# Reordering the side work of a delta-rule recurrence across the three phases of each step

## The chip, the cores and the metric

The kernel runs on one core of a Trainium2 chip. The metric is the device time of one execution in microseconds; where several runs are given, their median counts. A profiled execution also has a span, from the first to the last instruction in its trace, which is a little shorter than the time of the execution.

## The reference, cut to what matters

The reference is one post-norm encoder layer over 2048 tokens of 1024 channels. A single input projection feeds a gated long convolution (FFT) and an RWKV-7 mixer; the two are gated, projected and normed, and a SwiGLU network follows. The change lies in the RWKV-7 part, a recurrence over tokens that is run once in each direction:

```
def rwkv_step(S, inp):
    r, w, k, v, kk, a = inp
    sa = einsum('dbhvk,dbhk->dbhv', S, -kk)
    S = S * w[..., None, :] + sa[..., :, None] * (kk * a)[..., None, :] + v[..., :, None] * k[..., None, :]
    y = einsum('dbhvk,dbhk->dbhv', S, r)
    return S, y
...
_, ys = lax.scan(rwkv_step, S0, xs)
```

There are 8 heads with a 64 x 64 state each. The two directions are summed, normed per head, given a bonus term and a gate.

## The kernel before, in words

The kernel's stages follow one another on the core: projection of most columns with the preparation of the recurrence's operands beside it, then the recurrence (`chain`), the long convolution (`hyena`), the merge, and the feed-forward network. The projection's last 88 column blocks are kept back and computed inside the recurrence, as filler for TensorE; they are called the dense work here (tile `acc`, lines 202 to 204). One dense unit is three matmuls of 512 columns, and eight units make a block.

The recurrence works on chunks of 64 tokens: 32 chunks in each direction, N = 64 steps, in 8 groups of 8 steps (`g`, `st = divmod(n, 8)`). A step has three dependent products on TensorE, each followed by a copy on another engine:

- R: `pR` (line 803), the chunk's inputs against the state; ScalarE copies it to `R` (line 806). The step before then has its output product `pY` issued (`output`, lines 841 and 843).
- S: `pS` (line 816), the inverse `X` of the chunk's triangular matrix times `R`; ScalarE copies it to `SV` (line 819).
- D: `pD` (line 825), the state's change; VectorE adds and decays it into the next state (lines 831 and 832), which the next step's R needs.

`step` is a generator that yields after the R, the S and the D product. After each yield, `runs` issues some dense units (a share of the step's dense time: 0, a half, a half) and some of the step's side work, the parts that `beside` lists:

- `token_major(n + 1)`: four transposes for the next step's D (`pT`, line 786).
- `gram(g + 1, k)`: for each of the next group's eight chunks, 16 matmuls into two PSUM tiles of the tag `pg` (`pG`, line 677), then four masked copies on VectorE (line 656). Its input `ABp` is a DMA into one of three buffers, asked for when the third gram before it has been issued (line 667). Four grams stand in step 0 of a group and four in step 1 (`GRAMS`).
- `finish(g, hb)`: the correction that completes half of a group's inverses. A first product `pW1` (line 726) reads `XT` and the Gram tile `G`, two copies take it to `w1` (lines 733 and 734), and a second product `pW2` (line 739) reads `w1` and `X`. Half 0 (chunks 0 to 3) of the next group is finished in step 7, half 1 (chunks 4 to 7) in step 0 of the group itself. Half 0 also issues `states` for the next group's first chunk after `pW1`: two DMAs on SyncE's queue into `G` (line 781) that the first R of that group reads.
- `gated` (`pgg`, line 910) and `channel_major` (`pgt`, line 878): the output path, in the second direction alone.

All PSUM tiles of the side work share the tag `pg`, which has three buffers. The side work's parts are one list, and each phase runs down the list by cost: 0.34, 0.33 and 0.33 of the step's estimated cost, and what is left after the third. A step's dense time is a level minus the estimated cost of its side work (`share`), so that all steps come out about equally long.

After step 0 `gather(g + 1, 0)` and after step 1 `gather(g + 1, 1)` send the two halves of the Gram tiles through DRAM (GpSimd's queue, line 691). After step 1 `invert(g + 1)` follows: it loads `N` (line 701), runs a chain of 31 pairs of VectorE operations (lines 706 and 708), transposes the result into `XT` (line 713) and sends it through DRAM into `X` (lines 714 and 717). `XT` and `N` share one buffer.

The order of TensorE's instructions is the order in which the program issues them. The other engines' and the queues' order is planned when the program is built, by program order and the priorities given (`high_priority`).

The last three steps (n = 61 to 63; LAST is 61) have no dense work. At n = 61 `open` issues the loads for the convolution stage, and `step(61)` then issues `fetch(63)`, the last chunk's operands (`BK`, line 754); in steps 62 and 63 the side list ends with a part of the convolution's filters (`taps`, tiles `pg` and `pf`).

Of the kernel before, what the change touches and what calls it, by code (L numbers as in the profile page):

```python
# [25 lines left out]
NCH = L // CH  # L26
# [6 lines left out]
AHEAD = 1500  # L33
FIRST = 500
RUSH = 400
GRAMS = ((0, 1, 2, 3), (4, 5, 6, 7))
FX = 2
TB = 256

# [150 lines left out]
class Layer:  # L190
# [431 lines left out]
    def chain(self):  # L622
        tc, nc, i = self.tc, self.nc, self.i
        mm, tt, ts = nc.tensor.matmul, nc.vector.tensor_tensor, nc.vector.tensor_scalar
        NG, N = 8, 2 * NCH
        with tc.tile_pool(name="ch", bufs=1, reuse_waits="tile") as s, tc.tile_pool(name="chp", bufs=1, space=PSUM, reuse_waits="tile") as ps:
# [18 lines left out]
            def place(n):  # L645
                d, m = divmod(n, NCH)
                return d, (m if d == 0 else NCH - 1 - m)
# [72 lines left out]
            def finish(g, hb):  # L720
                G, XT, X = grp[g]["G"], grp[g]["XT"], Xs[g % 2]
                sl = slice(16 * hb, 16 * hb + 16)
                p1 = pg("pW1", (P, 16, 32))
                for n in range(16):
                    for j in range(2):
                        mm(p1[dn[j], n], G[up[j], j, 16 * hb + n, 32:64], XT[up[j], 16 * hb + n], start=True, stop=True)
                yield 0.55
                if g and hb == 0:
                    for j in range(2):
                        states(g * NG, j)  # L730
                w1 = s.tile([P, 16, 32], F32, name="w1", tag="w1", bufs=1)
                with tc.high_priority(offset=AHEAD):
                    nc.scalar.copy(w1[dn[0]], p1[dn[0]])
                    nc.vector.tensor_copy(w1[dn[1]], p1[dn[1]])
                yield 1.0
                p2 = pg("pW2", (P, 16, 32))
                for n in range(16):
                    for j in range(2):
                        mm(p2[up[j], n], w1[dn[j], n], X[dn[j], 16 * hb + n, 32:64], start=True, stop=True)
                yield 0.55  # L740
                with tc.high_priority(offset=AHEAD):
                    nc.scalar.copy(X[up[0], sl, 32:64], p2[up[0]])
                    nc.vector.tensor_copy(X[up[1], sl, 32:64], p2[up[1]])

            ins, VSs, T2s = {}, {}, {}
# [37 lines left out]
            def token_major(n):  # L783
                p = pg("pT", (P, HP, P))
                for hp in range(HP):
                    nc.tensor.transpose(p[:, hp], ins[n][0][:, hp], self.ident)
                    yield 0.11
                T2s[n] = s.tile([P, HP, P], F32, name="T2", tag="T2", bufs=2)
                with tc.high_priority(offset=AHEAD):
                    nc.scalar.copy(T2s[n], p)  # L790


            def step(n):
                d, c = place(n)
                g, st = divmod(n, NG)
                G, Gr, X = grp[g]["G"], grp[g]["Gr"][st], Xs[g % 2]
                BK, SV = ins.pop(n)
                VS = VSs.pop(n)
                T2 = T2s.pop(n)
                p = ps.tile([P, HP, 64], F32, name="pR", tag="pc", bufs=1)  # L800
                for hp in range(HP):
                    for j in range(2):
                        mm(p[opp[j], hp], G[:, j, HP * st + hp], VS[:, j, hp], start=True, stop=True)
                R = s.tile([P, HP, 64], F32, name="R", tag="R", bufs=1)
                with tc.high_priority(offset=AHEAD):
                    nc.scalar.copy(R, p)

                if late:
                    output(*late.pop())
                if n + 2 < N:  # L810
                    fetch(n + 2)
                yield 0.0, 0.34
                p = ps.tile([P, HP, 64], F32, name="pS", tag="pc", bufs=1)
                for hp in range(HP):
                    for j in range(2):
                        mm(p[opp[j], hp], X[opp[j], HP * st + hp], R[opp[j], hp], start=True, stop=True)
                with tc.high_priority(offset=AHEAD):
                    for j in range(2):
                        nc.scalar.copy(SV[opp[j], j], p[opp[j]])
                late.append((n, VS, SV, Gr))  # L820
                yield 0.5, 0.33
                pd = ps.tile([P, HP, 64], F32, name="pD", tag="pD", bufs=1)
                for hp in range(HP):
                    for j in range(2):
                        mm(pd[opp[j], hp], T2[:, hp, row[j]], SV[:, j, hp], start=True, stop=True)
                for j in range(2):
                    if (n + 1) % NCH == 0:
                        break
                    S1, q = VSs[n + 1][opp[j], j], opp[j]
                    with tc.high_priority(offset=AHEAD):  # L830
                        tt(out=S1, in0=pd[q], in1=VS[q, j], op=ALU.add)
                        tt(out=S1, in0=S1, in1=Dks[q, d, :, c:c + 1].broadcast_to([64, HP, 64]), op=ALU.mult)
                yield 0.5, 0.33

            def output(n, VS, SV, Gr):
                d, c = place(n)
# [111 lines left out]
            def beside(n, make=True):  # L948
                g, st = divmod(n, NG)
                parts = []  # L950
                if n + 1 < N:
                    parts.append((0.44, lambda: token_major(n + 1)))
                if n > NCH + 3 and n % 2 == 0:
                    parts.append((0.87, lambda: gated(place(n - 3)[1])))
                if g + 1 < N // NG:
                    for k in GRAMS[st] if st < len(GRAMS) else ():
                        parts.append((0.92, lambda k=k: gram(g + 1, k)))
                for hb, at in enumerate((NG - 1, 0)):
                    h = g + (at >= 4)
                    if st == at and 0 < h < N // NG:  # L960
                        parts.append((2.1, lambda h=h, hb=hb: finish(h, hb)))
                if n > NCH + 1:
                    parts.append((0.22, lambda: channel_major(place(n - 2)[1])))
                return sum(t for t, _ in parts), [f() for _, f in parts] if make else None

            costs = [beside(n, False)[0] for n in range(N)]

# [40 lines left out]

            owed = [0.0]

            def runs(need, aux, cost):
                owed[0] += need
                while need and owed[0] > 0.3:
                    t = next(more, None)
                    if t is None:
                        owed[0] = 0.0
                        break
                    left[0] -= t
                    owed[0] -= t
                while aux and cost > 0:  # L1020
                    t = next(aux[0], None)
                    if t is None:
                        aux.pop(0)
                    else:
                        cost -= t

            with tc.manual_schedule(engines={mybir.EngineType.PE}):
                begin(0)
# [18 lines left out]
                for n in range(N):  # L1047
                    g, st = divmod(n, NG)
                    if st == 0 and g + 1 < N // NG:
                        begin(g + 1)  # L1050
                    cost, aux = beside(n)
                    sh = share(n)
                    if n == LAST + 1:
                        taps = self.filt(0, 0)
                    if n >= LAST + 1:
                        aux.append(self.part(taps, 4.0))
                        cost += 4.0
                    outward(n)
                    if n > NCH + 2 and n % 2 == 1:
                        given(place(n - 2)[1])  # L1060
                    for k in range(n + 1, N if n >= LAST else min(n + 2, N)):
                        if k not in VSs:
                            near(k)
                    if n == LAST:
                        self.open()
                    for dense, other in step(n):
                        runs(sh * dense, aux, cost * other)
                    runs(0.0, aux, 1e9)
                    if n == LAST - 1:
                        for _ in more:  # L1070
                            pass
                    if n >= LAST and pieces:
                        self.taken(pieces.pop(0))
                    if st < len(GRAMS) and g + 1 < N // NG:
                        gather(g + 1, st)
                        if st:
                            invert(g + 1)
                output(*late.pop())
                for part in (gated(2), channel_major(1), channel_major(0), gated(0)):
# [50 lines left out]
    def next(self, name):  # L1130
        first, n = dict(w=(8, 2), g=(10, 2), A=(12, 2), B=(0, 2), H=(2, 3), Hs=(5, 3))[name]
        k = self.turns[name]
        self.turns[name] = k + 1
        return self.ring(first + k % n).rearrange("p (a b) -> p a b", b=P)
# [580 lines left out]
```

## Time and profile before

| what | us |
|---|---|
| median of 3 runs (lowest, highest) | 4027.47 (4022.36, 4030.42) |
| profiled execution, its time | 4030.92 |
| its span | 4029.1 |
| TensorE busy in the span | 3839.9 |
| recurrence's steps 0 to 60 in the trace, from and to | 746.5 to 1570.8 |

All times in the rows are counted from the start of the span. A busy TensorE is not TensorE at its peak: matmuls are pipelined, and their ends are modelled. The granted clock of TensorE stands as a share of full speed; 1.00 is 2.4 GHz and 0.50 is 1.2 GHz.

### The profile page before, as it was taken

The page shows a single profiled execution, that of the slowest core. Times are in us where ns is not written, and L with a number is a line of the kernel's source. Part 1 is how long each engine was busy: PE and PEld are TensorE (multiplying, and loading weights), DVE is VectorE, ACT ScalarE, POOL GpSimd, SP SyncE. Part 2 cuts the span into 40 slices and gives each one's busy share as a digit, 9 for nine tenths or more (in the row PEclk, how much of TensorE's full clock was granted, in tenths as well). Part 3 has the DMA queues.
Part 4 walks back from the last instruction along what each step waited for, and adds up shares of the span by engine and source line. Part 5 has one row for each costly group of instructions (what it writes and reads, how often), then busy time and mean ns, then how long its engine had stood idle before and what let it go on. Part 6 is the DMA issues. An engine that isn't in the chain of part 4 may idle for free. (4 is left out here: it accounts for less than half of the span.)

```text
span 4029.1 us, 64417 instructions
## 1 busy us (share of the span) xinstructions
PE 3839.9 (95%) x25872; PEld 3128.8 (78%) x25872; DVE 2422.1 (60%) x3823; ACT 1486.7 (37%) x2912; POOL 93.1 (2%) x139
## 2 busy tenths in 40 slices
PE   8999999899999998898888999999999999999998
PEld 6766557777777777788887899788888877888887
DVE  4456884666667774777876665544444464444444
ACT  3345662333335566665654333211111151111113
POOL 0000001111100000000000000000000000000000
PEclk9999999999999999899999999999999999999999
DMA  4556878676767766221225333411111132111111
GB/s 138 171 166 177 218 201 241 198 214 206 213 202 217 219 195 197 62 72 49 73 71 173 127 123 121 162 48 47 48 47 48 47 130 80 47 48 47 48 47 42
DMA packets 389698, 501.84 MB, mean 125 GB/s; under 512 B 135364, under 2 KB 271053, under 8 KB 388693
## 3 DMA queue, kind: packets, MB, share of 16 engines
q1 hardware_dynamic: 362775, 443.13, 36.7%
q10 hardware_dynamic: 20736, 37.80, 3.1%
q0 software_dynamic: 5888, 16.78, 1.4%
q8 instruction: 204, 3.34, 0.3%
q14 instruction: 95, 0.78, 0.1%
HBM read 352.74 MB, written 127.93 MB: 119 GB/s over the span
## 5 line engine op out<-in xcount | busy, mean ns | idle before, releaser
L202 PE MATMUL acc<-xh,wh 128*128 128x512 f32 x1376 | 580.1, 422 | 10.8 <-ACT xh L197 10.8
L203 PE MATMUL acc<-xl,wh 128*128 128x512 f32 x1376 | 550.1, 400 | 9.8 <-DVE xl L198 9.7
L204 PE MATMUL acc<-xh,wl 128*128 128x512 f32 x1376 | 549.5, 399 | 0.4 <-DVE wl L198 0.4
L1652 DVE TENSOR_TENSOR acc<-pd,acc 128x1024 f32<-128x1024 f32 x320 | 387.7, 1221 | 70.4 <-PE pd L204 64.5
L197 ACT CAST fwh<-raw 128x1024 fp32r<-128x1024 f32 x132 | 138.6, 1050 | 705.6 <-PE pg L203 488.9
L202 PEld LDWEIGHTS acc<-xh,wh 128*128 128x128 f32 x1376 | 261.2, 190 | 125.5 <-issue 48.6
L1680 DVE TENSOR_TENSOR h<-pu,sg 128x512 f32<-128x512 f32 x88 | 60.9, 692 | 492.0 <-PE pu L204 486.0
L203 PEld LDWEIGHTS acc<-xl,wh 128*128 128x128 f32 x1376 | 262.4, 191 | 73.0 <-DVE xl L198 13.6
L204 PEld LDWEIGHTS acc<-xh,wl 128*128 128x128 f32 x1376 | 262.0, 190 | 64.2 <-DVE wl L198 0.8
L202 PE MATMUL pd<-fwh,hh 128*128 128x512 f32 x704 | 276.3, 392 | 2.6 <-DVE acc L1650 2.2
L204 PE MATMUL pu<-fxh,fwl 128*128 128x512 f32 x704 | 277.5, 394 | 0.0
L204 PE MATMUL pg<-fxh,fwl 128*128 128x512 f32 x704 | 277.3, 394 | 0.0
L203 PE MATMUL pg<-fxl,fwh 128*128 128x512 f32 x704 | 276.2, 392 | 0.0
L202 PE MATMUL pg<-fxh,fwh 128*128 128x512 f32 x704 | 276.0, 392 | 0.2 <-DVE fxl L1567 0.2
L202 PE MATMUL pu<-fxh,fwh 128*128 128x512 f32 x704 | 275.3, 391 | 0.4 <-ACT fxh L1566 0.4
L203 PE MATMUL pu<-fxl,fwh 128*128 128x512 f32 x704 | 275.8, 392 | 0.0
L203 PE MATMUL pd<-fwl,hh 128*128 128x512 f32 x704 | 275.5, 391 | 0.0
L204 PE MATMUL pd<-fwh,hl 128*128 128x512 f32 x704 | 274.8, 390 | 0.0
L198 DVE TENSOR_TENSOR fwl<-raw,fwh 128x1024 fp32r<-128x1024 f32 x132 | 161.2, 1221 | 166.4 <-ACT fwh L197 162.5
L198 DVE TENSOR_TENSOR wl<-wraw,wh 128x512 fp32r<-128x512 f32 (+1 forms) x217 | 169.8, 791 | 136.1 <-ACT wh L197 125.0
L197 ACT CAST wh<-wraw 128x512 fp32r<-128x512 f32 (+1 forms) x217 | 150.7, 705 | 235.7 <-PE acc L203 202.3
L1221 DVE STREAM_TRANSPOSE V<-U 128x1024 f32<-128x1024 f32 x96 | 181.0, 1953 | 32.9 <-ACT U L1299 12.5
(299 smaller groups left out, 7583.0 us busy)
## 6 DMA issues: line engine op xcount, KB each, us to landing
wraw<-in_w_in SPq DMA_DIRECT2D x130, 512.0 KB, 5.0
ABp<-ABd SPq DMA_DIRECT2D x64, 512.0 KB, 5.8
raw<-in_fg SPq DMA_DIRECT2D x44, 512.0 KB, 3.4
raw<-in_fu SPq DMA_DIRECT2D x44, 512.0 KB, 3.5
raw<-in_fd SPq DMA_DIRECT2D x44, 512.0 KB, 3.5
ud<-ev ACTq DMA_DIRECT2D x84, 256.0 KB, 3.0
ABd<-AB SPq DMA_DIRECT2D x32, 512.0 KB, 5.0
gated<-ev SPq DMA_DIRECT2D x64, 256.0 KB, 2.8
```

The source lines that it names most:

```text
L197: nc.scalar.copy(hi, src)
L198: nc.vector.tensor_tensor(out=lo, in0=src, in1=hi.bitcast(F32), op=ALU.subtract)
L202: mm(ps, ah, bh, start=start, stop=False)
L203: mm(ps, ah, bl, start=False, stop=False)
L204: mm(ps, al, bh, start=False, stop=stop)
L1221: self.nc.vector.transpose(V[:, :, sl].rearrange("p j c -> p c j"), U[:, :, sl].rearrange("p n c -> p c n"))
L1652: tt(out=acc[t], in0=pf, in1=acc[t], op=ALU.add)
L1680: tt(out=h, in0=put, in1=sg, op=ALU.mult)
```

## The change

Each part of the side work is given a phase of its step. `beside` returns three lists, one for each phase, and `runs` issues the phase's dense units and then the whole of the phase's list. The estimated costs still set the dense time of a step, with 1.1 for a `finish` where 2.1 stood.

- The grams are spread as 3, 3 and 2 over steps 0, 1 and 2; steps 0 and 1 have one in each phase, step 2 one in phases 0 and 2.
- `finish` loses its first yield; its first product and the copies are in phase 1, its second product in phase 2. Half 1 moves from step 0 to step 2 of its group; half 0 stays in step 7.
- `token_major` is in phase 1, `channel_major` in phase 2, `gated` in phase 1 of steps with grams and in phase 0 of the others.
- The first gather stands after step 1, the second gather and `invert` after step 2.
- At n = 61 `fetch(63)` is issued ahead of `open`.
- In steps 62 and 63 the filters' part is split over the phases (0.8, 1.7, 1.7 where 4.0 stood at the list's end).

```diff
-GRAMS = ((0, 1, 2, 3), (4, 5, 6, 7))
+GRAMS = ((0, 1, 2), (3, 4, 5), (6, 7))
...
                         mm(p1[dn[j], n], G[up[j], j, 16 * hb + n, 32:64], XT[up[j], 16 * hb + n], start=True, stop=True)
-                yield 0.55
                 if g and hb == 0:
                     for j in range(2):
                         states(g * NG, j)
...
                     nc.vector.tensor_copy(w1[dn[1]], p1[dn[1]])
-                yield 1.0
+                yield 0.55
...
-                if n + 2 < N:
+                if n + 2 < N and n + 2 not in ins:
                     fetch(n + 2)
-                yield 0.0, 0.34
+                yield 0.0
...
+                put = lambda k, t, f: parts.append((k, t, f))
+                ks = GRAMS[st] if st < len(GRAMS) and g + 1 < N // NG else ()
+                for p, k in zip((0, 2) if len(ks) == 2 else (0, 1, 2), ks):
+                    put(p, 0.92, lambda k=k: gram(g + 1, k))
+
+                for hb, at in enumerate((NG - 1, 2)):
+                    h = g + (hb == 0)
+                    if st == at and 0 < h < N // NG:
+                        f = []
+                        put(1, 0.55, lambda h=h, hb=hb: f.append(finish(h, hb)) or until(f[0], 1))
+                        put(2, 0.55, lambda: f[0])
                 if n + 1 < N:
-                    parts.append((0.44, lambda: token_major(n + 1)))
+                    put(1, 0.44, lambda: token_major(n + 1))
+                if n > NCH + 1:
+                    put(2, 0.22, lambda: channel_major(place(n - 2)[1]))
                 if n > NCH + 3 and n % 2 == 0:
-                    parts.append((0.87, lambda: gated(place(n - 3)[1])))
...
-                return sum(t for t, _ in parts), [f() for _, f in parts] if make else None
+                    put(1 if ks else 0, 0.87, lambda: gated(place(n - 3)[1]))
+                total = sum(t for _, t, _ in parts)
+                return total, [[f() for k, _, f in parts if k == p] for p in range(3)] if make else None
+
+            def until(gen, n):
+                for _ in range(n):
+                    yield next(gen)
...
-                while aux and cost > 0:
-                    t = next(aux[0], None)
-                    if t is None:
-                        aux.pop(0)
-                    else:
-                        cost -= t
+                for gen in aux:
+                    for _ in gen:
+                        pass
...
-                        aux.append(self.part(taps, 4.0))
-                        cost += 4.0
+                        for p in range(3):
+                            aux[p].append(self.part(taps, 1.7 if p else 0.8))
...
                     if n == LAST:
+                        fetch(n + 2)
                         self.open()
-                    for dense, other in step(n):
-                        runs(sh * dense, aux, cost * other)
-                    runs(0.0, aux, 1e9)
+                    for dense, other in zip(step(n), aux):
+                        runs(sh * dense, other)
...
-                    if st < len(GRAMS) and g + 1 < N // NG:
-                        gather(g + 1, st)
-                        if st:
+                    if 0 < st < len(GRAMS) and g + 1 < N // NG:
+                        gather(g + 1, st - 1)
+                        if st > 1:
                             invert(g + 1)
```

## Rows read from the trace of the kernel before

**Rows 1.** The page: span, and TensorE's busy time in it.
```profile
span 4029.1 us, 64417 instructions
PE 3839.9 (95%) x25872; PEld 3128.8 (78%) x25872; DVE 2422.1 (60%) x3823; ACT 1486.7 (37%) x2912; POOL 93.1 (2%) x139
```

**Rows 2.** Busy time by stretch (then clock, DMA share): group 1; steps 0-60; the end.
```profile
854.00:959.60 105.60, 101.55 (x1302) 81.62 (x1298) 64.82 (x152) 34.95 (x74) 10.55 (x16) 1.00 0.69 204
...
746.50:1570.80 824.30, 783.34 (x9744) 634.11 (x9743) 538.41 (x1322) 371.20 (x970) 72.78 (x110) 0.98 0.71 209
1570.80:1629.50 58.70, 37.44 (x430) 33.18 (x430) 32.79 (x71) 46.67 (x125) 0.00 (x0) 0.80 0.54 168
```

**Rows 3.** TensorE's groups of instructions, 746 to 1570 us: busy, mean ns, idle before.
```profile
L203 PE MATMUL acc<-xl,wh 128*128 128x512 f32 x602 | 239.3, 397 | 5.7 <-DVE xl L198 5.6
...
L677 PE MATMUL pG<-ABp 64*128 64x128 f32 x896 | 73.6, 291 | 24.4 <-DVE rg L656 20.8 <-DMA ABp<-ABd 3.6
...
L739 PE MATMUL pW<-X,w 32*32 32x32 f32 x896 | 18.9, 195 | 5.9 <-DVE w L734 4.0 <-issue 1.9
```

**Rows 4.** Timeline of step 16, its second and its fourth gram: start, length, what.
```profile
963.79 1.13 PE L677 MATMUL pG<-ABp 64*128 64x128 f32 x14 [0.71 <-DVE rg L656]
...
969.37 1.25 PE L677 MATMUL pG<-ABp 64*128 64x128 f32 x16 [1.16 <-DMA ABp<-ABd]
```

**Rows 5.** Stretches at half clock in steps 24, 32/33 and 49, columns as Rows 2.
```profile
1070.20:1076.90 6.70, 5.75 (x43) 4.69 (x45) 2.56 (x8) 0.73 (x2) 0.00 (x0) 0.50 0.79 226
1189.70:1196.40 6.70, 6.44 (x120) 5.80 (x122) 1.69 (x4) 1.55 (x4) 0.00 (x0) 0.50 0.48 131
...
1414.90:1418.30 3.40, 3.40 (x52) 2.97 (x52) 1.35 (x4) 1.49 (x4) 0.00 (x0) 0.50 0.53 143
1428.60:1431.90 3.30, 3.30 (x30) 2.77 (x28) 1.70 (x5) 0.00 (x0) 1.48 (x3) 0.50 0.88 259
```

**Rows 6.** Timeline of step 11, which has no gram, from R to S.
```profile
897.62 0.37 ACT L806 COPY R<-pR 128x256 f32<-128x256 f32 x1
...
898.17 0.29 PE L843 MATMUL pY<-SV,rg 128*64 128x64 f32 x4
...
898.75 0.68 PE L816 MATMUL pS<-R,X 64*64 64x64 f32 x16
```

**Rows 7.** Timelines of TensorE and SyncE's queue in step 15: finish, states.
```profile
949.36 1.20 PE L726 MATMUL pW<-XT,G 32*32 32x32 f32 x64
...
950.99 2.05 SPq L781 DMA_DIRECT2D G<-ABd  x2
...
959.56 0.69 PE L803 MATMUL pR<-VS,G 128*64 128x64 f32 x16
```

**Rows 8.** Timelines of GpSimd, VectorE and TensorE: the last group's inverse.
```profile
1430.22 1.29 POOL L691 DMA_DIRECT2D Nd<-G  x2 [18.53 <-DVE G L656]
...
1482.42 4.07 DVE L713 STREAM_TRANSPOSE XT<-W 32x1024 f32<-32x1024 f32 x2
...
1487.88 3.17 POOL L717 DMA_DIRECT2D X<-Wd  x4 [4.38 <-DMA Wd<-W]
...
1498.75 1.20 PE L726 MATMUL pW<-XT,G 32*32 32x32 f32 x64
...
1507.09 1.20 PE L739 MATMUL pW<-X,w 32*32 32x32 f32 x64
```

**Rows 9.** DMA issues, 746 to 1570 us: KB each, median us to landing.
```profile
G<-ABd SPq DMA_DIRECT2D x115, 64.0 KB, 3.9
...
Wd<-W POOLq DMA_DIRECT2D x7, 512.0 KB, 4.1
X<-Wd POOLq DMA_DIRECT2D x28, 128.0 KB, 5.5
```

**Rows 10.** Timelines of SyncE's queue and TensorE at step 62: the last operands.
```profile
1580.29 0.56 SPq L754 DMA_DIRECT2D BK<-ABd  x1
...
1585.44 1.12 PE L786 MATMUL pT<-k_c_ident,BK 128*128 128x128 f32 x4 [6.18 <-DMA BK<-ABd]
```

More of the change, by code (lines that the diff above doesn't have):

```diff
@@ L820, in step @@
                 late.append((n, VS, SV, Gr))
-                yield 0.5, 0.33
+                yield 0.5
                 pd = ps.tile([P, HP, 64], F32, name="pD", tag="pD", bufs=1)
@@ L832, in step @@
                         tt(out=S1, in0=S1, in1=Dks[q, d, :, c:c + 1].broadcast_to([64, HP, 64]), op=ALU.mult)
-                yield 0.5, 0.33
+                yield 0.5
             def output(n, VS, SV, Gr):
@@ L950, in beside @@
                 parts = []
+                put = lambda k, t, f: parts.append((k, t, f))
[8 more added lines that the diff above has]
+                        put(2, 0.55, lambda: f[0])
                 if n + 1 < N:
-                    parts.append((0.44, lambda: token_major(n + 1)))
+                    put(1, 0.44, lambda: token_major(n + 1))
+                if n > NCH + 1:
+                    put(2, 0.22, lambda: channel_major(place(n - 2)[1]))
                 if n > NCH + 3 and n % 2 == 0:
-                    parts.append((0.87, lambda: gated(place(n - 3)[1])))
[L955 to L963, printed above, removed]
-                return sum(t for t, _ in parts), [f() for _, f in parts] if make else None
+                    put(1 if ks else 0, 0.87, lambda: gated(place(n - 3)[1]))
[4 more added lines that the diff above has]
+                    yield next(gen)
             costs = [beside(n, False)[0] for n in range(N)]
@@ L1009, in chain, with runs @@
             owed = [0.0]
-            def runs(need, aux, cost):
+            def runs(need, aux):
                 owed[0] += need
```

## The prediction, made before the changed kernel ran

> **What bounds the kernel now.** I read the page first: TensorE is busy 95% of the span [rows 1], so time is won where it stands still or runs slowly. I then cut the trace by stage, since the change touches the recurrence alone. Steps 0 to 60 take 824.3 us with TensorE busy for 783.3, so 41 us of idle lie there; VectorE has 538 and the DMA engines a share of 0.71, and neither is the bound. The end of the recurrence, 58.7 us after it, has TensorE busy for only 37.4 [rows 2]. The groups of TensorE's instructions say in front of what the 41 us stand: 24.4 before the grams, 5.9 before the second product of the correction, 5.7 before the dense work where its token block changes [rows 3]. The grams' wait is for VectorE's masked copies (20.8) and for `ABp` (3.6): a gram takes two of the three `pg` buffers, so a gram right behind another must wait until the first is copied out (0.71 us at the second gram of step 16), and the fourth of a step comes before its input has been fetched (1.16) [rows 4]. Last, the granted clock: four stretches in or just behind steps with grams stand at 0.50, that is 1.2 GHz, after TensorE had run the small products of a gram step with waits between them; they sum to 20.1 us [rows 5].
>
> So the recurrence is bound by TensorE's own work, with bunched side work that makes it wait. Some 36 of its 41 us of idle stand at those three places; the steps without a gram and a block change have next to none, and nothing can be won there.
>
> **The change part by part.** The work is the same before and after: as many grams, transposes, corrections and dense units. Only idle time, clock and new waits count. The sum is made against the profiled execution (4030.9 us; its span is 4029.1), which lies 3.4 us above the median of 4027.5.
>
> *Grams, one in each phase.* Between two grams now stand either R and Y or S or D with half of the step's dense time. With a gram directly behind another the buffer was 0.71 us late [rows 4]; R and Y alone are longer than that (R's copy, which starts behind R, starts 1.13 us before S [rows 6]). So the waits of 20.8 go nearly whole. The input: in step 16 it was asked for within the step that used it, and was 1.16 us late; now three grams lie between, a whole step of some 13 us (a group's 105.6 us over eight steps [rows 2]); the 3.6 go. What is late next is the token transpose or `gated` behind a gram of the same phase, which need a third and fourth buffer: I leave 2 us for that. Gain 24.4, at least 12 (if half of the copies are still behind other work of VectorE), at most 24.4; cost 2.
>
> *The correction in two phases.* `pW2` stood right behind `w1`'s copies in step 0, where only a minimum of dense work was left between; now D and half the dense time are between. The 5.9 us [rows 3] go; bounds 4 to 5.9. Its first product stays without a wait.
>
> *The clock.* 20.1 us at half speed cost 10 us of work. After the change no phase of a gram step lacks dense work except phase 0, and the waits between its products are gone. Some dips may stay or appear at other places, so I take 6; bounds -4 (one more dip of 6.7 us, at half speed, costs 3.4) and 10.
>
> *Phase 0 without filler.* In a step without a gram, phase 0 now has only R and Y before S; two transposes move to phase 1. ScalarE's copy of R ends at 897.99 in step 11, while Y's last matmuls start at 898.17 and S at 898.75 [rows 6]. The copy is done before Y is, so S starts earlier and does not wait: nothing, with Y as the cover. The cover is 0.18 us and more; if ScalarE first ends another copy as long as this one (0.37), it falls short by 0.2 us, 61 times at worst: bounds -12 and +5 (for fewer switches between kinds of matmul).
>
> *Half 0 in step 7: the states behind it.* `pW1` moves from phase 0 to phase 1, and `states` with it. SyncE's queue issues its two DMAs 1.63 us after `pW1` begins, the pair takes 2.05 us [rows 7], and such a DMA lands 3.9 us after its issue [rows 9]: 7.6 us in all, before the next group's R may start. Today R starts 10.2 us after `pW1` [rows 7]. That stretch holds both corrections (1.2 each), S and D (0.7 each, as R's row has it) and nine dense units, so a unit is some 0.7 us. Afterwards it holds both corrections, the transposes (0.5, by the two that stand with Y's end in the 0.58 us before S [rows 6]), D and five dense units: 1.2 + 0.5 + 0.7 + 3.6 + 1.2 = 7.2. R is late by 0.4 us, seven times: cost 3; bounds 0 and 17 (2.4 each, when SyncE, which waits in order, is 2 us behind). Behind these two on SyncE stand the next operands, which are wanted two steps later.
>
> *The inverse one step later.* Gather and `invert` start a step later, some 13 us, and the first product that needs them only 3 us later in step 7 (10.2 against 7.2). In the last group `XT` is ready at 1486.5 (1482.42 and 4.07) and read at 1498.75 [rows 8]: 12.3 us to spare become 2. The second product needs `X`: its four DMAs end their issue at 1491.1 and land 5.5 us later [rows 9], the first two about 1495, and the product starts at 1507.09 [rows 8]: 12 us to spare become about -1, as it stays at the end of the step. On TensorE's queue D's successor R and all that follows stand behind such a wait. I take 0.6 us a group, cost 4; bounds 0 and 35 (5 us in each).
>
> The Trainium skill has a price for these transfers: its page DMA: Bandwidth & Descriptors, section Anatomy of one DMA (SWDGE path), gives a GpSimd DMA about 2.0 us fixed and the bytes at 436 GB/s on top, an estimate of 3.2 us for `Wd` and 2.3 for `X`. The trace has 4.1 and 5.5 [rows 9], so it does not agree, and the measurement decides. By the page the chain would be some 4 us shorter and the cost of this edit 0, which would make the forecast 3991.
>
> *The end.* The last `BK` is issued at 1580.29, and TensorE waits 6.18 us for it at 1585.44 [rows 10]. Issued ahead of `open` it is early, and the wait goes. Late next are the filters' inputs, which are on the same queue, and their chain over ScalarE and VectorE, which leaves TensorE idle for 21 of the 58.7 us [rows 2]. I take 5; bounds 0 and 8 (the stretch runs at a clock of 0.80).
>
> *The block changes* (5.7 [rows 3]) fall on the same steps as before, by the shares that the code works out: 0; bounds -5 and +5.
>
> Sum: 24.4 + 5.9 + 6 + 5 = 41.3 of gain, 2 + 3 + 4 = 9 of cost, net 32. The profiled execution would take 3998.6, and the median, 3.4 below, 3995.
>
> **The rivals.** (a) The inverse decides: slower. Its chain is VectorE's, whose order is planned anew; for it speaks that a margin of 12 us is used up by a delay of 13, against it that VectorE has a third of the stage free and that a chain moved as a whole keeps its length. TensorE, in order, then waits in step 7 of each group with `pW1` or `pW2` at the head. The price is the lateness times seven, and from 5 us a group (35) it eats the gain. With 8 us a group and a clock dip each (3.4) it is 80 against 36 of other net gain: 4027.5 + 44 = 4071; with 6 us and a dip in half of the groups, 4046.
>
> (b) The buffers still decide: the change spreads the grams, but the planned order of VectorE puts masked copies behind the weights' splits or the inverse, so half of the grams' waits (12 us) stay, and the clock gains 3 less: net 17, 4010. For it: three buffers for gram, transposes and output in one phase. Against: 0.71 us was the wait with the copies directly behind [rows 4], and dense time now lies between.
>
> (c) All idle time turns into other idle time: states, inverse and block changes at the upper middle of their bounds (8 + 15 + 5) with the end's gain 0: about 4023, no change.
>
> (d) Everything goes and nothing comes: the clock gives 10, the end 8, the costs are 0, switches give 3: 24.4 + 5.9 + 10 + 8 + 3 = 51, 3976.
>
> **How the numbers follow.** Forecast 0.60 (its own range 3983 to 4006), (d) 0.14, (b) 0.12, (a) 0.08, (c) 0.06. Two in ten are left out at most when the range reaches from just below (d) to past (b): 3973 to 4018. About 0.2%, 8 us, is what can be told from no change. Faster by more: the forecast, (d) and (b) are, 0.86. Within: (c) and a small part of (a), 0.07. Slower: the rest of (a), 0.07.
>
> **What would show it.** In the changed kernel's trace, the idle time before `pG` should be 0 to 4 us and that before `pW` in the corrections below 5; TensorE's idle in steps 0 to 60 should fall from 41 to about 17 (states, inverse and block changes); that stretch should take about 797 us. Of the clock's half-speed stretches between steps 0 and 60, at most two should be left. The wait for `BK` should be gone and the stretch from step 61 to the end of the recurrence be some 5 us shorter. R of steps 8, 16 and so on waiting for a DMA into `G` shows the states' term; `pW` waiting for `XT` or `X` shows the inverse's. The prediction is wrong if grams still wait, if waits in step 7 pass 15 us in sum, or if TensorE comes to wait in front of S, for 0.2 us a step or more.

## The result, and the profile after

| | before | changed |
|---|---|---|
| median, us (lowest to highest, runs) | 4028.94 (4022.36 to 4037.11, 4) | 3991.18 (3981.09 to 3993.05, 4) |
| profiled execution, us | 4030.92 | 3990.72 |

The ratio is 0.990, with an interval of 0.9875 to 0.9925: faster by 1.0%, about 38 us; 3995 was forecast. The two traces, cut by stage:

| stage, us | before | after | TensorE idle | at half clock |
|---|---|---|---|---|
| up to step 0 | 746.5 | 743.7 | | |
| steps 0 to 60 | 824.3 | 793.0 | 41.0 -> 21.4 | 27.3 -> 14.7 |
| step 61 to the end of the recurrence | 58.7 | 51.3 | 21.3 -> 13.6 | |
| the rest | 2399.6 | 2400.9 | | 64.9 -> 76.6 |

The last column is the time of the stretch, busy or not, in which the granted clock was 0.50. Nearly all of the gain lies in the two middle rows, where the change is. The first and last are code that was not changed; over all executions read here the rest took 2392 to 2408 us and had 55 to 104 us at half clock, so a whole time can't resolve a few us, and the experiments below are read by stage.

Busy time by stretch in the changed kernel, against [rows 2]: steps 0 to 60, the end, and the two stretches at half clock that hold 13.6 of the 14.7 us (columns as there).

```profile
743.70:1536.70 793.00, 771.64 (x9744) 625.21 (x9743) 535.37 (x1322) 373.00 (x972) 72.80 (x110) 0.99 0.74 217
1536.70:1588.00 51.30, 37.70 (x429) 33.27 (x429) 27.58 (x64) 44.81 (x122) 0.00 (x0) 0.80 0.59 182
1069.10:1072.50 3.40, 3.40 (x19) 2.70 (x15) 1.45 (x5) 0.73 (x2) 2.57 (x4) 0.50 0.92 281
1253.40:1263.60 10.20, 8.27 (x94) 6.77 (x95) 4.52 (x7) 1.16 (x2) 4.28 (x6) 0.50 0.72 186
```

The same 9744 matmuls take TensorE 11.7 us less, and 19.6 us of idle time are gone. The kernel before also had a fifth stretch at half clock, beside the four of [rows 5]; it lies in step 37, where the token block changes:

```profile
1261.30:1268.10 6.80, 3.67 (x47) 3.03 (x49) 4.77 (x6) 1.84 (x4) 3.10 (x4) 0.50 0.60 201
```

TensorE was busy for about 23 us of the time at half clock before and for about 13 after, so some 5 of the 11.7 us are the clock's. In front of what TensorE still stands idle is told by its groups of instructions from 743 to 1537 us (busy, mean ns, idle before), against [rows 3]:

```profile
L202 PE MATMUL acc<-xh,wh 128*128 128x512 f32 x601 | 252.3, 420 | 1.4 <-ACT wh L197 1.2
...
L203 PE MATMUL acc<-xl,wh 128*128 128x512 f32 x602 | 239.8, 398 | 1.1 <-DVE xl L198 1.1
L677 PE MATMUL pG<-ABp 64*128 64x128 f32 x896 | 66.7, 285 | 0.7 <-PE pY L842 0.5 <-DVE rg L656 0.2
...
L802 PE MATMUL pR<-VS,G 128*64 128x64 f32 x987 | 44.8, 230 | 4.2 <-issue 2.6 <-PE acc L204 0.9
...
L815 PE MATMUL pS<-R,X 64*64 64x64 f32 x976 | 42.1, 225 | 6.5 <-ACT R L805 5.6 <-DVE nm L859 0.9
...
L726 PE MATMUL pW<-XT,G 32*32 32x32 f32 x896 | 18.3, 195 | 6.5 <-DVE XT L713 6.5
L738 PE MATMUL pW<-X,w 32*32 32x32 f32 x896 | 17.0, 192 | 0.2 <-DMA X<-Wd 0.2
```

The grams' 24.4 us have become 0.7 and the second product's 5.9 have become 0.2. New are 6.5 before the first product, which waits for `XT`. Three groups of before have no row above: from 746 to 1571 us its trace has these idle times before R, S and the dense work's first matmul.

```profile
L202 PE MATMUL acc<-xh,wh 128*128 128x512 f32 x601 | 251.8, 419 | 2.0 <-ACT xh L197 2.0
...
L803 PE MATMUL pR<-VS,G 128*64 128x64 f32 x978 | 44.0, 233 | 0.8 <-issue 0.5
...
L816 PE MATMUL pS<-R,X 64*64 64x64 f32 x976 | 42.0, 226 | 1.0 <-ACT R L806 1.0
```

So S went from 1.0 to 6.5 and R from 0.8 to 4.2, while the dense work went from 7.7 (2.0 and 5.7) to 2.7. Part of the wait at S is the block change in another place, as the changed kernel's timeline of step 3 shows (start, length, what):

```profile
780.82 0.46 PE L802 MATMUL pR<-VS,G 128*64 128x64 f32 x10
...
782.27 1.05 ACT L197 CAST xh<-xraw 128x1024 fp32r<-128x1024 f32 x1
783.22 0.36 ACT L805 COPY R<-pR 128x256 f32<-128x256 f32 x1
...
783.64 0.68 PE L815 MATMUL pS<-R,X 64*64 64x64 f32 x16 [1.42 <-ACT R L805]
```

R's products were done about 781.3, but ScalarE had a cast of the next token block (1.05) ahead of R's copy. The block changes in steps 3 and 37, and these two steps have 2.6 of the 6.5 us at S. The other 3.9 stand in steps 25, 39 and 44, behind ScalarE's casts of weights and other work, and in step 56, behind VectorE. The small idle before R is VectorE's counterpart, in step 14: the transposes into `XT` hold the engine for 4.07 us, a split of weights comes next, and only then D's update of the state, for which R waits.

```profile
928.22 4.07 DVE L713 STREAM_TRANSPOSE XT<-W 32x1024 f32<-32x1024 f32 x2
932.14 1.25 DVE L198 TENSOR_TENSOR wl<-wraw,wh 128x512 fp32r<-128x512 f32 x2
933.43 0.88 DVE L830 TENSOR_TENSOR VS<-pD,VS 64x256 f32<-64x256 f32 x2
934.34 0.87 DVE L831 TENSOR_TENSOR VS<-VS,Dks 64x256 f32<-64x256 f32 x2
...
934.86 1.02 PE L802 MATMUL pR<-VS,G 128*64 128x64 f32 x15 [0.69 <-issue]
```

### The profile page after: what moved, and what is told of

Its sections match the earlier page's. It is cut to its first block, busy times and chain, and to the rows that moved or that the text cites. A ratio compares the mean times of both kernels' runs of the same rounds, so it can differ in the third digit from the quotient of the medians.

```text
span 3988.9 us, 64402 instructions
## 1 busy us (share of the span) xinstructions
PE 3830.1 (96%) x25872; PEld 3122.5 (78%) x25872; DVE 2419.7 (61%) x3823; ACT 1487.5 (37%) x2914; POOL 93.1 (2%) x139
## 5 line engine op out<-in xcount | busy, mean ns | idle before, releaser
L1226 DVE STREAM_TRANSPOSE V<-U 128x1024 f32<-128x1024 f32 x96 | 180.9, 1951 | 29.6 <-ACT U L1304 12.4
```

The lines of the kernel that those rows point to most:

```text
L1226: self.nc.vector.transpose(V[:, :, sl].rearrange("p j c -> p c j"), U[:, :, sl].rearrange("p n c -> p c n"))
```

## The experiments

All are edits of the changed kernel, with the same work unless said. Times are medians, ratios are to the kernel before on the same chip with their interval; steps and end are from the one profiled execution of each.

| kernel | time | ratio | steps 0-60 | idle there | half clock there | end |
|---|---|---|---|---|---|---|
| before | 4028.94 | 1 | 824.3 | 41.0 | 27.3 | 58.7 |
| changed | 3991.18 | 0.990 (0.9875-0.9925) | 793.0 | 21.4 | 14.7 | 51.3 |
| e1_bunched | 3995.49 | 0.9921 (0.9899-0.9944) | 803.5 | 29.6 | 18.3 | 51.8 |
| e9_bunched_fin0 | 3995.39 | 0.9934 (0.9912-0.9955) | 802.6 | 31.6 | 13.7 | 51.1 |
| e12_spread_fin0 | 3995.78 | 0.9929 (0.9908-0.9951) | 802.5 | 27.5 | 30.7 | 51.3 |
| e3_one_phase | 3997.32 | 0.9916 (0.9891-0.9941) | 800.8 | 21.4 | 37.5 | 49.9 |
| e6_token_first | 3990.11 | 0.9916 (0.9888-0.9944) | 797.1 | 21.1 | 17.1 | 49.3 |
| e2_late_fetch | 3990.26 | 0.9902 (0.9882-0.9922) | 790.4 | 19.6 | 17.9 | 50.9 |
| e10_taps_last | 3993.07 | 0.9923 (0.9899-0.9947) | 797.0 | 22.3 | 23.9 | 56.2 |
| e4_invert_later | 3986.56 | 0.9900 (0.9869-0.9930) | 797.9 | 25.2 | 17.1 | 51.7 |
| e7_small_turns | 3984.59 | 0.9898 (0.9873-0.9922) | 796.8 | 22.6 | 20.5 | 52.9 |
| e8_gram_later | 4036.97 | 1.0038 (1.0024-1.0052) | 845.2 | 60.2 | 75.9 | 51.2 |
| e5_grams_first | 3980.58 | 0.9884 (0.9848-0.9920) | 788.2 | 18.3 | 13.7 | 51.9 |
| e11_first_and_last | 3984.59 | 0.9899 (0.9876-0.9922) | 784.9 | 15.0 | 17.1 | 48.3 |

The yardstick for a stage: e2, e4, e7 and e10 leave the order of TensorE's work in steps 0 to 60 as it is. With the changed kernel that is five executions, 790.4 to 797.9, mean 795.0. Every other kernel is read from one execution, so a difference of a few us from the mean is not told from that scatter.

### Grams bunched again, and the correction's second half back in step 0

```diff
 e1, e9:
-GRAMS = ((0, 1, 2), (3, 4, 5), (6, 7))
+GRAMS = ((0, 1, 2, 3), (4, 5, 6, 7), ())
-                for p, k in zip((0, 2) if len(ks) == 2 else (0, 1, 2), ks):
+                for p, k in zip((0, 0, 1, 2), ks):
 e9, e12:
-                for hb, at in enumerate((NG - 1, 2)):
+                for hb, at in enumerate((NG - 1, 0)):
```

> The changed kernel with its grams bunched again: four in step 0 and four in step 1 of a group, in phases 0, 0, 1 and 2; all else as changed (correction in two phases, half 1 and the inverse after step 2, early fetch). If the spreading of the grams is what pays: the idle time before pG goes from 0.7 us back to 15 to 24 us in steps 0 to 60, with one or more further stretches at half clock behind gram steps, and the kernel takes 20 to 30 us longer than the changed one, about 0.995 to 0.998 of the kernel before. If the spreading is not it and the gain came with the other edits or with the dense time's new shares: idle before pG under 8 us, and the time within 8 us of the changed kernel (0.990).

> The changed kernel with the grams bunched again and half 1's correction back in step 0, in phases 1 and 2 there. With e1 (bunched, correction in step 2: 15.0 us idle before pG) and e12 it makes a table of two by two. If the two edits meet in step 0, where the correction's cost takes the dense time away from between the grams: 20 to 26 us idle before pG, as in the kernel before (24.4), and 5 to 15 us longer than e1. If the rest of the 24.4 us came from how phases were filled before (by cost, parts running together): 13 to 17 us before pG, and the time of e1.

> The changed kernel with its grams spread, but half 1's correction in step 0 again, in phases 1 and 2. If the spread alone keeps a gram clear of the one before: under 4 us idle before pG and before pW2, and the time within 8 us of the changed kernel. If the correction in step 0 brings the buffers' wait back (a gram, a correction product and a transpose in phase 1): 5 to 12 us before pG, pW and pT together, and 5 to 15 us longer. The inverse starts some 1 us earlier, since step 2 is shorter, so its wait for XT should be 5 us or less.

The group of grams (busy, mean ns, idle before), in e1, e9 and e12:

```profile
L677 PE MATMUL pG<-ABp 64*128 64x128 f32 x896 | 69.3, 287 | 15.0 <-DVE rg L656 15.0
```

```profile
L677 PE MATMUL pG<-ABp 64*128 64x128 f32 x896 | 67.9, 284 | 13.1 <-DVE rg L656 11.3 <-DVE X L742 1.8
```

```profile
L677 PE MATMUL pG<-ABp 64*128 64x128 f32 x896 | 65.6, 285 | 0.2 <-DVE rg L656 0.2
```

Two grams in one phase wait for 13 to 15 us in all, spread ones for under 1, wherever the correction stands. So the buffer's mechanism is shown. Why it is 13 to 15 and not the 24.4 of before is told by the order of the products: filling by cost, the kernel before had two pairs of grams with nothing between in each of its 14 gram steps, the first with the second and the third with the fourth. The lists of e1 and e9 bring back only the first pair. Step 16 in e9 (the second, third and fourth gram), against before's in [rows 4]:

```profile
958.50 1.13 PE L677 MATMUL pG<-ABp 64*128 64x128 f32 x14 [0.72 <-DVE rg L656]
...
961.76 1.16 PE L677 MATMUL pG<-ABp 64*128 64x128 f32 x16
...
966.78 1.16 PE L677 MATMUL pG<-ABp 64*128 64x128 f32 x16
```

The second gram waits as before (0.71), the fourth, which stands alone now, no longer (1.16). In all gram steps of the kernel before, 11.6 of the 24.4 us stand in front of the second gram and 12.7 in front of the fourth. So e1 and e9 are half of the old bunching, and they bring back about half of its wait; the spreading accounts for the whole.

In time e1 missed: 20 to 30 us more were expected, and its steps are 8.5 us over the mean of 795.0. The two edits don't add either: each taken back alone gives 802.5 to 803.5, both together 802.6. With one execution of each it is not shown that the 7.5 us are won only with both. Why e12 is slower, without a wait of the grams, is not settled: it has 7.9 us of idle before R, 8.0 before the first product, and twice the time at half clock.

### The second half's two products in one phase

```diff
-                        put(1, 0.55, lambda h=h, hb=hb: f.append(finish(h, hb)) or until(f[0], 1))
-                        put(2, 0.55, lambda: f[0])
+                        put(1 + hb, 0.55, lambda h=h, hb=hb: f.append(finish(h, hb)) or until(f[0], 1))
+                        put(2, 0.55, lambda f=f: f[0])
```

> The changed kernel with half 1's correction in one phase: pW2 stands right behind pW1 and its copies, in phase 2 of step 2, seven times. If it was the copies between the two products that TensorE waited for: idle before pW2 of 0.7 to 1.0 us seven times, 5 to 7 us in all, and the kernel about 5 us longer than the changed one. If what mattered was that step 0 had next to no dense time: idle before pW2 under 2 us, since step 2 has more of it, and the time unchanged.

```profile
L738 PE MATMUL pW<-X,w 32*32 32x32 f32 x896 | 19.2, 195 | 8.1 <-ACT w L732 4.7 <-DVE w L733 3.3
```

With nothing between the products, the second waits for both copies in each of the seven groups: 8.1 us, against 0.2. The sum of idle did not rise, since in this execution the wait for `XT` was 1.2 and R's 0.1; but TensorE ran 37.5 us at half clock, and the stretch is 5.8 us over the mean. The term of the correction is shown. In e9 and e12, where the correction is back in step 0 but in two phases, the second product does not wait either.

### The inverse

```diff
 e4, e8:
-                    if 0 < st < len(GRAMS) and g + 1 < N // NG:
-                        gather(g + 1, st - 1)
+                    if st in (1, 3) and g + 1 < N // NG:
+                        gather(g + 1, st // 2)
 e8 as well:
-GRAMS = ((0, 1, 2), (3, 4, 5), (6, 7))
+GRAMS = ((0, 1, 2), (3, 4, 5), (6,), (7,))
-                for p, k in zip((0, 2) if len(ks) == 2 else (0, 1, 2), ks):
+                for p, k in zip((2,) if st == 3 else (0, 1, 2), ks):
 e5 alone:
+                for p, k in zip((0, 1, 2), ks):
```

> The changed kernel with the second gather and the inverse one step later still (after step 3). If the inverse now ends at the edge, as its waits of 6.5 us before pW1 in steps 39, 47 and 55 say, the margin of 0 to 8 us is overrun by a step's 12 us: idle before pW of 4 to 12 us in nearly each of the seven groups, 45 to 85 us in all, stretches at half clock behind it, and the kernel 50 to 100 us longer than the changed one, slower than the kernel before. If the inverse still has room and those three waits come from VectorE's other work in these steps: idle before pW under 20 us, and the kernel less than 20 us longer than the changed one.

> The changed kernel with the eighth gram moved from phase 2 of step 2 to phase 2 of step 3, and the gather and the inverse behind it, so that the inverse starts a whole step later (some 12 us). This is the slower rival's mechanism at its own dose. XT is ready 8 to 9 us before pW1 in the first four groups and 1 to 3 us too late in the last three of the changed kernel. If TensorE, in order, then pays each us of lateness: idle before pW of about 4 us in four groups and 13 us in three, 45 to 65 us in all, with several stretches at half clock, and the kernel 45 to 80 us longer than the changed one, slower than the kernel before. If the waits are spread by slack elsewhere (VectorE's chain running faster in other steps): idle before pW under 25 us, and less than 25 us longer.

> The changed kernel with step 2's second gram in phase 1 in place of phase 2, some 6 us earlier; the run with the inverse's call moved one step showed that the call's place in the program does not set its start, so this theory is that the last gram's masked copies do. If so, the gather and the inverse start 5 to 6 us earlier in every group, the wait of pW1 for XT in steps 39, 47 and 55 goes from 6.5 us to under 1.5, and the kernel gains 4 to 8 us over the changed one. If the inverse's start is set elsewhere (by the load's place in GpSimd's queue or the planned order of VectorE), the first operation of the inverse moves by less than 2 us and the wait stays over 4 us. A gram, a correction product and a transpose in one phase may cost 0.7 us each time on the three buffers, 5 us in all.

e4 missed: it moves the call of `invert` to a step later in the program, and the first operation stays where it was. The load of `N` with which an inverse begins, from GpSimd's timelines of the kernel before, the changed kernel, e4, e8 and e5:

```profile
780.60 0.58 POOL L701 DMA_DIRECT2D N<-Nd  x1 [5.34 <-PE acc L204]
```

```profile
792.67 0.58 POOL L701 DMA_DIRECT2D N<-Nd  x1 [6.47 <-PE acc L204]
```

```profile
791.54 0.58 POOL L701 DMA_DIRECT2D N<-Nd  x1 [6.48 <-PE acc L204]
```

```profile
803.89 0.58 POOL L701 DMA_DIRECT2D N<-Nd  x1 [5.65 <-DMA Nd<-G]
```

```profile
787.26 0.58 POOL L701 DMA_DIRECT2D N<-Nd  x1 [7.02 <-DMA Nd<-G]
```

From step 0 of each (746.5, 743.7, 742.8, 744.0 and 744.7) that is 34.1, 49.0, 48.7, 59.9 and 42.6 us. What sets it is the last gram: a step later it is 11 us later, one phase earlier it is 6 us earlier. And this is the slower rival. In e8 the first product waits for `XT` in every group, up to 10.7 us, and in each of these seven steps stands a stretch at half clock, of 6.8 to 17.1 us:

```profile
L726 PE MATMUL pW<-XT,G 32*32 32x32 f32 x896 | 23.8, 214 | 52.9 <-DVE XT L713 52.9
```

The stretch grows by 50 us over the mean, and the kernel is slower than before (1.0038). In e5 that wait is gone, and others stand in its place: 1.5 us for the transfer into `X`, 2.2 before the transposes that now follow a gram and a product, and 9.8 for R's copy:

```profile
L815 PE MATMUL pS<-R,X 64*64 64x64 f32 x976 | 42.3, 227 | 9.8 <-ACT R L805 9.8
L726 PE MATMUL pW<-XT,G 32*32 32x32 f32 x896 | 17.0, 192 | 1.0 <-DVE nm L860 1.0
L738 PE MATMUL pW<-X,w 32*32 32x32 f32 x896 | 17.0, 192 | 1.5 <-DMA X<-Wd 1.5
```

```diff
 e7:
-                        nc.vector.transpose(XT[q].rearrange("p n i -> p i n"), W[q])
+                        for b in range(0, 32, 8):
+                            nc.vector.transpose(XT[q].rearrange("p n i -> p i n")[:, b:b + 8], W[q][:, b:b + 8])
```

> The changed kernel with each of the two transposes that make XT on VectorE (2.0 us each) cut into four of 0.5 us. In steps 6, 14, 22 and 30 the state's update stands behind the pair (4.07 us) and R waits 0.4 to 0.9 us for it, 2.6 to 3.7 us in all. If the length of the pair is the cause and the planned order lets the update pass between the parts: R's waits fall under 1.5 us, and the kernel gains 1 to 4 us, within what can be told. If the planned order keeps the eight parts together: R's waits stay the same or grow by the parts' fixed cost (some 0.5 us a group).

Next to nothing moved: before R 3.1 us (4.2), before the first product 6.5 (6.5). The planned order keeps the pieces together, and in step 14 the eight hold VectorE for 4.07 us, as long as the two did.

### The end

```diff
 e2:
                     if n == LAST:
-                        fetch(n + 2)
                         self.open()
 e10:
-                        for p in range(3):
-                            aux[p].append(self.part(taps, 1.7 if p else 0.8))
+                        aux[2].append(self.part(taps, 4.0))
```

> The changed kernel with the last chunk's operands fetched behind the convolution's loads again. If the early fetch gave the end's gain: TensorE waits some 4 to 6 us for BK again, the stretch from step 61 to the convolution's first transposes goes from 51.3 to 56 to 59 us, and the kernel takes 5 to 7 us longer than the changed one. If the end's gain came from the filters' new split over the phases: no wait for BK over 2 us, the stretch within 2 us of 51.3, the time unchanged.

> The changed kernel with the filters' part of steps 62 and 63 in one piece at the end of phase 2, the early fetch kept. The run with the late fetch kept the end at 50.9 us, so the fetch did not give the end's gain. If the split of the filters' part did: the stretch from step 61 to the convolution's first transposes goes from 51.4 to 55 to 59 us. If either of the two edits is enough: the stretch stays within 2 us of 51.4.

TensorE's waits in the end: of the changed kernel, of e2 and of e10 (in all, times, longest):

```profile
PE pgt L877 <- ACT y L869: 6.8, 5, 3.2
PE pg L1206 <- DMA H3b<-H3d: 3.6, 1, 3.6
PE pg L1206 <- DVE rg L1210: 1.3, 1, 1.3
```

```profile
PE pgt L877 <- ACT y L869: 6.8, 5, 3.2
PE pT L785 <- DMA BK<-ABd: 2.7, 1, 2.7
```

```profile
PE pgt L877 <- ACT y L869: 8.7, 6, 4.2
PE pg L1205 <- ACT rg L1204: 3.1, 1, 3.1
PE pD L824 <- ACT SV L818: 2.5, 2, 2.2
```

Without the early fetch the wait for `BK` is back, at 2.7 us, the one for a filter's input is gone, and the end is as short (50.9). The wait is not the 6.18 of before: the transposes that read `BK` begin 7.9 us after the first R product of step 62, against 8.6 before, but they stand behind S now, and TensorE has S and a part of the filters to do meanwhile. With the fetch early but the filters' part in one piece at the end of each step, the wait for `BK` stays away, yet the end is 56.2: ScalarE's copies are waited for instead. All the other kernels, with the part split, have 48.3 to 52.9. So filters at the end of a step cost some 5 us.

That is not what the split gave over the kernel before, though. Filling by cost, that kernel had spread the filters' products over the step as well, as its trace of step 62 shows:

```profile
1589.45 0.94 PE L1201 MATMUL pg<-fw,H3b 128*128 128x128 f32 x6
1590.32 0.68 PE L816 MATMUL pS<-R,X 64*64 64x64 f32 x16
1590.93 1.16 PE L1201 MATMUL pg<-fw,H3b 128*128 128x128 f32 x8
...
1593.80 0.69 PE L825 MATMUL pD<-SV,T 128*64 128x64 f32 x16
1594.42 1.16 PE L1191 MATMUL pf<-rg,Fc 128*128 128x128 f32 x8
```

What is shown is that the new order of the last steps makes the end shorter without the early fetch. Which part of the order does it, and whether the early fetch alone would have helped the old one, was not run.

### Filler in phase 0, and a version further

```diff
 e6:
-                    put(1, 0.44, lambda: token_major(n + 1))
+                    put(1 if ks or (n > NCH + 3 and n % 2 == 0) else 0, 0.44, lambda: token_major(n + 1))
 e11, with e5's line for the grams:
+                    put(2 if len(ks) == 2 else 1, 0.44, lambda: token_major(n + 1))
```

> The changed kernel with the token transposes in phase 0 in the steps that have neither a gram nor a gated part there, so that TensorE has 0.45 us more to do between Y and S. TensorE waits 6.5 us in front of S in the changed kernel (1.0 before). If it is the missing filler, the wait falls to 1 to 4 us, and the steps without a gram take 0.1 us more for the extra change of the kind of matmul, 30 times: the time within 5 us of the changed kernel. If the wait is for ScalarE being taken by casts of over 1 us, as in the block changes, it stays over 4 us.

> A version meant to beat both: the changed kernel with step 2's second gram in phase 1 (as in e5) and its token transposes in phase 2, away from the gram. In e5 TensorE no longer waited for XT (6.5 us before), but 1.9 and 0.4 us before the transposes and 1.0 before gated in that phase. Expected: no wait for XT over 1 us, those before pT under 0.5 us, steps 0 to 60 of 784 to 790 us, and 4 to 12 us less than the changed kernel, 0.986 to 0.990 of the kernel before. If the waits in front of S (9.8 us in e5) come from the earlier inverse, they stay, and the time is within 4 us of the changed kernel.

In e6 TensorE waits 6.9 us before S in all (6.5 without the edit). But 4.9 of them stand in steps 25, 44 and 56, which have a gram or a `gated` part and which the edit leaves as they were. The others stand in steps 3, 37 and 39, with the transposes before S again:

```profile
783.91 0.68 PE L815 MATMUL pS<-R,X 64*64 64x64 f32 x16 [1.32 <-ACT R L805]
...
1223.91 0.68 PE L815 MATMUL pS<-R,X 64*64 64x64 f32 x16 [0.23 <-ACT R L805]
...
1249.27 0.68 PE L815 MATMUL pS<-R,X 64*64 64x64 f32 x16 [0.41 <-ACT R L805]
```

The changed kernel has 1.42 in step 3 (shown above) and these in steps 37 and 39:

```profile
1221.10 0.68 PE L815 MATMUL pS<-R,X 64*64 64x64 f32 x16 [1.22 <-ACT R L805]
...
1247.01 0.68 PE L815 MATMUL pS<-R,X 64*64 64x64 f32 x16 [1.11 <-ACT R L805]
```

That is 2.0 us against 3.8, and against 3.4 to 4.4 in the yardstick's five. So filler covers part of ScalarE's work ahead of R's copy, but not the cast of a token block in step 3. It costs something too: TensorE's busy time, less half of the busy time at half clock, is 769.1 in e6, against 762.6 to 765.6 in the five executions of the yardstick and 771.9 before. The same matmuls take some 5 us less with the transposes behind S, by this one execution; why is not shown. The stretch itself (797.1) lies within the yardstick's.

e11 has the shortest steps (784.9, 10 us under the mean) and 15.0 us of idle, with no wait for `XT`; its waits before S stayed (8.5). Its whole time is not to be told from the changed kernel's; the same holds of e5.

## Why the prediction was right, point by point

- **What bounds it**: shown. The gain came mostly from idle time and clock at the places named, and 38.7 of the 40.2 us that the span lost lie in steps 0 to 60 and the end. The steps gave 31.3 (29.3 by the yardstick's mean), where the terms without the end's sum to 27; the end gave 7.4 instead of 5.
- **Grams**: 24.4 to 0.7, with 2 left in the forecast. Size and cause were right: two grams in one phase wait, spread ones don't, and the kernel before had two such pairs a gram step.
- **Correction**: 5.9 to 0.2, as said, and e3 shows it. The second product did not stand right behind the copies in step 0, though: D and one or two dense units lay between, and it waited even so. That the first product stays without a wait was wrong there, but stands in the inverse's term.
- **Clock**: the time at half clock fell by 12.6, of which TensorE was busy for 10: 5 us of work, against 6. The working's 20.1 us left out the fifth stretch, which stands at a block change and not at a gram. The yardstick's five have 14.7 to 23.9 us, with TensorE busy for 12.8 to 21.5, against 22.9 before, so 1 to 5 is what can be claimed. One of the two dips left begins at the end of the wait for `XT`: at 1253.7 the first product had waited 3.0 us.
- **The inverse one step later**: mis-sized. The cost was set at 4; it is 6.5 before the first product, about 3 before R behind the transposes, which was not foreseen, and a dip of 10.2 us at half clock in this execution, with TensorE busy for 8.27 of it: 4 us more. The delay was 15 us (34.1 to 49.0 after step 0) and not 13. Idle before `pW` was to be below 5 and is 6.7, so that sign failed. The forecast let the second product wait for `X`'s DMA, by 12 us of margin become -1; it was the first, whose margin was put at 2, and the second waited 0.2. The rival's condition was right: e8 shows that a further 11 us make the kernel slower than before.
- **States**: a cost of 3 was set aside, and R waits for no DMA into `G` in the changed kernel; it does in e11, 2.1 us once.
- **Phase 0 without filler**: costed at nothing, with the switches as the better bound. That bound was nearer: some 5 us by e6's one execution. Y as the cover falls short where ScalarE has other work ahead of R's copy, as the term's lower bound had said: 6.5 us before S, 0.11 a step, below the 0.2 that would have refuted it.
- **Block changes**: 0 was set. In steps 3 and 37 the dense work and S waited 8.7 us together before and 5.1 after, a gain of 3.6 within the bounds. Over all steps the sum is about the same (8.7 and 9.2) only because S waits 3.9 in other steps, which belongs to phase 0.
- **The end**: the term's size was about right (5 against 7.4), but the step behind it failed: "Issued ahead of `open` it is early, and the wait goes" is true, and yet without the early fetch the end is as short. Another wait stood ready behind `BK`'s (3.6 for the filter's input), as the working had feared. The new order of the last steps, which the working had not priced, makes the end shorter; its parts were not run apart.

The Trainium skill's rule in the working (DMA: Bandwidth & Descriptors, Anatomy of one DMA (SWDGE path)) would have set the inverse's cost at 0. In the changed kernel `Wd` lands after 3.8 us and `X` after 4.6 in the median, against 3.2 and 2.3 as estimates from the page; the DMAs ended only 0.2 us of the waits, so the rule decided nothing here.

The size came out close partly by luck. Of the 31.3 us in the steps, 19.6 are idle time (the terms give 21.3), 5 the clock (6), and the other 6.7 are time of the matmuls that the sum put at nothing. Two sums of the working are off: idle of 17 was to be left, where its terms give 19.7 (21.4 was measured), and the terms of rival (c) add up to about 4021, not 4023.

## What to carry to other kernels

Where side work shares a few buffers with engines that must drain them, give each phase of the main chain one user of the buffers, and put dense work between two dependent small products: on an engine that runs in order, both show as idle time in front of the second. A chain on another engine that the planner places starts when its last input is ready, not where the program calls it; to start it earlier, move that input, and price its lateness by the first reader at the head of the in-order engine. And when a wait goes and a stage gets shorter, undo the one edit and then the other before writing down which did it, and look in the trace whether the undone edit brings back the old order: e1, e9 and e10 did so only in part.

## What the runs showed that was not expected

- Undoing either of two edits alone cost about the same 7.5 us as undoing both (802.5, 803.5 and 802.6 against 795.0), in one execution of each.
- The same matmuls cost less in the new order: corrected for the clock, TensorE is busy for 771.9 us before and 762.6 to 765.6 in the five with the changed order. By the groups' busy time most of it lies in the grams: they take 73.6 us in the kernel before with two pairs a gram step, 69.3 and 67.9 in e1 and e9 with one, and 66.7 in the changed kernel with none (some of the 73.6 is at half clock). So a wait seems to cost more than the idle time that it shows, which no run shows apart.
- Code that was not changed varied by 16 us between executions (2392 to 2408), with 55 to 104 us of it at half clock.
